# Two PSUM banks of the attention logits for the first products behind a k-outer group, and products and weight splits pinned to their pair or head chunk

## The chip, the cores and the metric

The kernel runs on one core of a Trainium2 chip. The metric is the device time of one execution in microseconds (us), lower is better: 987.88 us is the median of three runs of the kernel before (987.56 to 987.98).

## The reference

Two transformer blocks over 256 tokens of width 1024, in float32. The first mixes by a linear recurrence, gated linear attention and block-sparse attention, and ends in a SwiGLU with 2816 hidden units (22 columns of 128). The second has a convolution layer and an attention layer, each followed by a SwiGLU of the same size, with shifts, scales and gates from a vector c (adaLN). Cut to what matters here:

```python
def first_block(x, ...):
    x = x + rms_norm(hybrid_mixer(rms_norm(x, g0), ...) @ w_out, g1)
    h = rms_norm(x, g2)
    f = (silu(h @ w_ffn_gate) * (h @ w_ffn_up)) @ w_ffn_down          # ffn0
    return x + rms_norm(f, g3)

def second_block(x, c, ...):
    for l in range(2):
        sh1, sc1, g1, sh2, sc2, g2 = split(silu(c) @ w_ada[l] + b_ada[l], 6)
        h = x * (1 + sc1) + sh1
        if l == 0:
            gb, gc, v = split(h @ w_in, 3)                             # conv
            y = (gb * conv3(gc * v)) @ w_out
        else:
            k, v, F = shared_kv(x, c, ...)                             # F: cumulated log forget gates
            logits = q @ k.T / 8 + F[t] - F[s]                         # causal, 16 heads
            y = (softmax(logits) @ v) @ w_o                            # FoX
        x = layer_norm(alpha * x + g1 * y, ...)
        h = x * (1 + sc2) + sh2
        y = (silu(h @ w_gate) * (h @ w_up)) @ w_down                   # ffn1, ffn2
        x = layer_norm(alpha * x + g2 * y, ...)
    return x
```

## The kernel before

All activations lie transposed: 8 tiles of 128 features x 256 tokens. A float32 product is made of three matmuls on TensorE (PE): a weight block of 128 x 128 is split into a high part wh and a low part wl, the activation into xh and xl (yh, yl and mh, ml elsewhere), and wh·xh, wl·xh and wh·xl are summed in PSUM (`mm3`, L162 to L164; `ksteps`, L197 to L203). Weights come in tiles of 128 x 1024 (512 KB, eight blocks): the SP queue loads `raw` (L127, 4 buffers), ScalarE (ACT) casts it to `wh` (L144) and VectorE (DVE) subtracts to get `wl` (L150); wh and wl have 5 buffers each. One such tile feeds 24 matmuls, which this text calls a block of PE work.

PSUM has eight banks, in three pools: `acc` 4, `lg` 2 and `ms` 2. `lg` holds the attention logits and the target of the warm-up products (`warm`, L331), `ms` statistics, broadcasts and transposes. Where a layer's input becomes ready tile by tile, `kouter` computes eight columns at once with the eight k-steps outside, in all four acc banks. After that, columns come one after the other: `pair` (a gate and an up column in one bank, 48 matmuls) in the SwiGLUs, `single` elsewhere. `evac` in `ffn` multiplies silu(gate) and up (L918; in ffn0 with a scaling first, L909 and L911, then L914), and splits the result into mh (L921, ACT) and ml (L922, DVE). Columns j of a SwiGLU after the k-outer group start at n + 4, n being the columns computed ahead (0 in ffn0, 3 in ffn1 and ffn2). In conv the eight columns of the group are the first of the order c, v, b of head 0, head 1 and so on; L1207 ff. take the others by `single`, and L1212, L1215 evacuate.

adaLN: silu(c) @ w_ada is done on DVE, a row of 1024 products with a running sum each (`gw`, L371, from a load of 512 KB, 3 buffers, L368). There are 112 of them, spread over the program by `fill` and `drain`.

The program is written in stages and a scheduler orders the instructions of each engine; what the text adds by hand are order-only dependencies (`after`). A gw comes behind the last wl that was emitted (`self.anchor`) and behind `self.gbound`, if set. `unbroken(ins, free)` sets `self.bound`: after `free` more weight tiles, each wl comes behind an instruction of `ins`; it sets gbound to the last of them.

FoX works through the 16 heads in eight chunks of two. For chunk i: the query columns of chunk i + 1 (`wq`), logits of chunk i (L773 to L781) in the two lg banks, the transposes of chunk i - 1 (`fox_pt`, L805 to L807, a_pt), two k-steps of the output projection (`step`, `out`), and the softmax of chunk i (`fox_softmax`): a maximum on DVE (L793), the exps on ACT with a running sum (L794), a reciprocal (L795) and the scaling a_L (L797). Its PE order is the program's. Before the loop all wl's are pinned behind one instruction, and after chunk 0 behind that and chunk 0's last maximum:

```python
                if i == 0:
                    self.unbroken([self.gbound, self.mxs], 0)
```

Of the kernel before, what the change touches and what calls it, by code (L numbers as in the profile page):

```python
# [9 lines left out]
F32 = mybir.dt.float32  # L10
# [4 lines left out]
ALU = mybir.AluOpType  # L15
AX = mybir.AxisListType

P = 128
D = 1024
T = 256  # L20
NK = D // P
# [43 lines left out]
class Net:  # L65
# [99 lines left out]
        if self.strict:  # L165
            self.chain(m)

    def single(self, wname, c, X, nk=NK, fill=True):
        t = self.acc([P, T])
        for k in range(nk):  # L170
            self.mm3(t, wname, k, c, X[0][k], X[1][k], k == 0, k == nk - 1)
        if fill:
            self.fill(nk / NK)
        return t

    def pair(self, w0, c0, w1, c1, X):
        t = self.acc([P, 2, T])
        for j, (w, c) in enumerate(((w0, c0), (w1, c1))):
            for k in range(NK):
                self.mm3(t[:, j, :], w, k, c, X[0][k], X[1][k], k == 0 and j == 0, k == NK - 1 and j == 1)  # L180
        self.fill(2)
        return t
# [601 lines left out]
    def fox_softmax(self, lg):  # L784

        V, A = self.nc.vector, self.nc.scalar
        mx = self.tmp("a_mx", (P, 4))
        sm = self.tmp("a_sm", (P, 4))
        Ls = [self.tmp("a_L", (P, 384), bufs=4) for _ in range(2)]
        part = [(hh, j, s) for hh in range(2) for j, s in ((0, slice(0, T)), (1, slice(T, 384)))]  # L790
        for hh, j, s in part:
            c = slice(2 * hh + j, 2 * hh + j + 1)
            self.mxs = V.tensor_reduce(mx[:, c], lg[hh][:, s], AX.X, ALU.max, negate=True)  # L793
            self.fn = A.activation(Ls[hh][:, s], lg[hh][:, s], AF.Exp, bias=mx[:, c], accum_out=sm[:, c])  # L794
        V.reciprocal(sm, sm)  # L795
        for hh, j, s in part:
            V.tensor_scalar(Ls[hh][:, s], Ls[hh][:, s], sm[:, 2 * hh + j:2 * hh + j + 1], None, ALU.mult)  # L797
        return Ls

    def fox_pt(self, Ls):  # L800
# [99 lines left out]
    def ffn(self, l, X, R=None, first=(), rows=None):  # L900

        nc = self.nc
        V = nc.vector
        MH, ML = [], []

        def evac(g, u):
            if R is not None:
                g2 = self.tmp("ff_g")
                V.tensor_tensor(g2, g, R, ALU.mult)  # L909
                u2 = self.tmp("ff_u")  # L910
                V.tensor_tensor(u2, u, R, ALU.mult)  # L911
                s = self.silu(g2)
                m = self.tmp("ff_m")
                V.tensor_tensor(m, s, u2, ALU.mult)  # L914
            else:
                s = self.silu(g)
                m = self.tmp("ff_m")
                V.tensor_tensor(m, s, u, ALU.mult)  # L918
            h = self.tl(self.fp, [P, T + 2], "mh", F32R)[:, 0:T]
            lo = self.tl(self.fp, [P, T + 2], "ml", F32R)[:, 0:T]  # L920
            nc.scalar.activation(h, m, AF.Copy)  # L921
            V.tensor_tensor(lo, m, h.bitcast(F32), ALU.subtract)  # L922
            MH.append(h)
            ML.append(lo)

        wg, wu = f"g{l}", f"u{l}"
        n = len(first) // 2
        for o in range(0, 2 * n, 4):
            outs = [self.tmp("ff_g" if q % 2 == 0 else "ff_u") for q in range(o, min(2 * n, o + 4))]
            self.lazy_outs(first[o:o + 4], *rows, outs)  # L930
            for j in range(0, len(outs), 2):
                evac(*outs[j:j + 2])
        for ps in self.kouter([(w, n + j) for j in range(4) for w in (wg, wu)], X, False):
            evac(ps[:, 0, :], ps[:, 1, :])
        for j in range(n + 4, NFF):
            ps = self.pair(wg, j, wu, j, X)
            self.drain()
            evac(ps[:, 0, :], ps[:, 1, :])
        return MH, ML
# [139 lines left out]
    def run(self):  # L1079
        nc = self.nc  # L1080
        V, A, G = nc.vector, nc.scalar, nc.gpsimd
# [6 lines left out]
        X = ([], [])  # L1088
# [58 lines left out]
        X = Y  # L1147
# [54 lines left out]
        got = {}  # L1202
# [4 lines left out]
        for i in range(NK):  # L1207
            for w in ("ci_c", "ci_v", "ci_b"):
                if (w, i) not in got:
                    got[(w, i)] = self.single(w, i, X)  # L1210
            c = self.tmp("c_c")
            A.activation(c, got[("ci_c", i)], AF.Copy)  # L1212
            up = self.tmp("c_up", (P, T + 2))
# [87 lines left out]
            for j, t in enumerate(self.fox_pv(i, pts, vs)):  # L1301
                Y[j].append(t)

        self.unbroken([self.gbound], 2)
        with self.tc.manual_schedule(engines={nc.tensor.engine}):
            q = wq(0)
            Ls = None
            step, pre = self.partial("wo")
            for i in range(NK + 1):
                qn = wq(i + 1) if i < NK - 1 else None  # L1310
                lg = self.fox_logits(i, q, ks[i]) if i < NK else None
                pts = self.fox_pt(Ls) if i else None
                if i > 1:
                    step(Y, i - 2)
                if i:
                    out(i - 1, pts)
                Ls = self.fox_softmax(lg) if i < NK else None
                if i == 0:
                    self.unbroken([self.gbound, self.mxs], 0)
                q = qn  # L1320
                self.drain()
            step(Y, NK - 1)
# [162 lines left out]
```

## Time and profile before

| | before |
|---|---|
| median of three runs | 987.88 us (987.56 to 987.98) |
| profiled execution | 985.9 us, of which the span of instructions is 984.2 |
| PE busy | 927.9 us, 94% |
| DVE busy | 768.8 us, 78% |
| ACT busy | 530.2 us, 54% |

The profile is of one execution. A row of a timeline gives start and length in us, engine, line, operation, what it writes and reads, and in brackets how long its engine stood idle before it and which instruction released it. Matmuls overlap, so their lengths are longer than their spacing. The granted clock is TensorE's, as a part of 2.4 GHz.

### The profile page before, as it was taken

To read this page: it belongs to the slowest core of one execution; us is meant where nothing else is said; L and a number is where in the kernel's file an instruction comes from. 1 tells how busy PE (TensorE), PEld (TensorE's weight loads), DVE (VectorE), ACT (ScalarE), POOL (GpSimd) and SP (SyncE) were. 2 spreads that over 40 slices of the span, in tenths; PEclk is the share of its full clock that TensorE was granted. 3 is DMA by queue.
4 is the path that set the end of the run, shared out by engine and by line. 5 is a ranking of instruction groups with operands and counts; after the bars stand their busy time and mean duration, and the time that the engine had idled before them with its cause. 6 is when DMAs were issued, how large, how long until landed. Compare 5 with 4: busy or idle time off the path is not lost.

```text
span 984.2 us, 19003 instructions
## 1 busy us (share of the span) xinstructions
PE 927.9 (94%) x7434; PEld 893.6 (91%) x7434; DVE 768.8 (78%) x1471; ACT 530.2 (54%) x951; POOL 19.7 (2%) x66
## 2 busy tenths in 40 slices
PE   7989997999999999998899999999699999999996
PEld 7879896999999899998899999987587899999995
DVE  7896678999988588679899899796764897665553
ACT  7484653554444555548555454377365586554331
POOL 1111000000000000000000000000000000000001
PEclk9999998999999999999999999999799999999998
DMA  8754337899999477544999999454642257655531
GB/s 291 249 197 129 108 108 278 294 330 327 318 336 390 142 255 250 179 134 155 320 341 356 329 368 348 167 176 145 250 150 65 87 153 275 214 184 183 191 108 43
DMA packets 62346, 219.56 MB, mean 223 GB/s; under 512 B 7112, under 2 KB 8784, under 8 KB 62256
## 3 DMA queue, kind: packets, MB, share of 16 engines
q1 hardware_dynamic: 61056, 215.06, 63.7%
q0 software_dynamic: 1056, 3.16, 1.0%
q8 instruction: 58, 0.95, 0.4%
q14 instruction: 32, 0.26, 0.1%
q10 hardware_dynamic: 144, 0.13, 0.0%
HBM read 217.26 MB, written 2.63 MB: 223 GB/s over the span
## 4 chain that ended last, share of the span: by engine, by line
PE 80%; DVE 12%; ACT 4%; issue 3%; DMA 2%; DVEq 0%; ACTq 0%
PE acc L162 20%; PE acc L164 20%; PE acc L163 20%; PE acc L197 4%; DVE wl L150 4%; PE acc L198 4%; PE acc L203 3%; DMA raw<-wts 1%; ACT wh L144 1%; DVE gw L371 1%; PE acc L251 1%; PE acc L253 1%; PE acc L252 1%; PE ms L820 1%; PE lg L773 1%
## 5 line engine op out<-in xcount | busy, mean ns | idle before, releaser
L150 DVE TENSOR_TENSOR wl<-raw,wh 128x1024 fp32r<-128x1024 f32 (+2 forms) x296 | 356.2, 1209 | 102.4 <-ACT wh L144 101.0
L144 ACT ACTIVATE wh<-raw 128x1024 fp32r<-128x1024 f32 (+2 forms) x296 | 307.6, 1046 | 225.4 <-PE acc L164 128.2
L162 PE MATMUL acc<-yh,wh 128*128 128x256 f32 x608 | 171.1, 282 | 7.0 <-DVE ff_m L918 5.6
L162 PE MATMUL acc<-xh,wh 128*128 128x256 f32 x576 | 164.2, 285 | 8.9 <-DVE ff_u L911 7.2
L164 PE MATMUL acc<-yl,wh 128*128 128x256 f32 x608 | 171.3, 282 | 0.0
L163 PE MATMUL acc<-yh,wl 128*128 128x256 f32 x608 | 170.6, 281 | 0.0
L163 PE MATMUL acc<-xh,wl 128*128 128x256 f32 x576 | 162.9, 283 | 1.4 <-DVE wl L150 1.4
L164 PE MATMUL acc<-xl,wh 128*128 128x256 f32 x576 | 163.0, 283 | 0.0
L163 PE MATMUL acc<-mh,wl 128*128 128x256 f32 x528 | 148.1, 281 | 0.0
L164 PE MATMUL acc<-ml,wh 128*128 128x256 f32 x528 | 148.1, 281 | 0.0
L162 PE MATMUL acc<-mh,wh 128*128 128x256 f32 x528 | 147.9, 281 | 0.0
L371 DVE SCALAR_TENSOR_TENSOR gw<-gw,cact 128x1024 f32<-128x1024 f32 x112 | 134.7, 1221 | 0.6 <-DMA gw<-ada 0.4
L162 PEld LDWEIGHTS acc<-yh,wh 128*128 128x128 f32 x608 | 115.2, 190 | 7.6 <-DVE ff_m L918 6.1
L162 PEld LDWEIGHTS acc<-xh,wh 128*128 128x128 f32 x576 | 109.9, 191 | 11.3 <-DVE ff_u L911 7.4
L163 PEld LDWEIGHTS acc<-yh,wl 128*128 128x128 f32 x608 | 115.2, 190 | 0.4 <-issue 0.4
L164 PEld LDWEIGHTS acc<-yl,wh 128*128 128x128 f32 x608 | 114.9, 189 | 0.6 <-issue 0.6
L163 PEld LDWEIGHTS acc<-xh,wl 128*128 128x128 f32 x576 | 110.1, 191 | 1.8 <-DVE wl L150 1.6
L164 PEld LDWEIGHTS acc<-xl,wh 128*128 128x128 f32 x576 | 109.8, 191 | 0.1
L162 PEld LDWEIGHTS acc<-mh,wh 128*128 128x128 f32 x528 | 99.5, 189 | 0.0
L164 PEld LDWEIGHTS acc<-ml,wh 128*128 128x128 f32 x528 | 99.4, 189 | 0.0
L163 PEld LDWEIGHTS acc<-mh,wl 128*128 128x128 f32 x528 | 99.3, 188 | 0.0
L197 PE MATMUL acc<-xh,wh 128*128 128x256 f32 (+1 forms) x256 | 67.7, 294 | 8.7 <-ACT wh L144 5.5
(399 smaller groups left out, 1493.2 us busy)
## 6 DMA issues: line engine op xcount, KB each, us to landing
raw<-wts SPq DMA_DIRECT2D x288, 512.0 KB, 4.5
gw<-ada SPq DMA_DIRECT2D x112, 512.0 KB, 5.6
raw<-wts SPq DMA_DIRECT2D x6, 256.0 KB, 5.9
m_scr<-m_row POOLq DMA_DIRECT2D x2, 768.0 KB, 5.8
ax<-xT SPq DMA_DIRECT2D x4, 256.0 KB, 4.8
m_b<-m_scr POOLq DMA_DIRECT2D x8, 128.0 KB, 3.6
out<-fg SPq DMA_DIRECT2D x8, 128.0 KB, 1.8
cst<-cst SPq DMA_DIRECT2D x1, 588.5 KB, 7.1
```

Source lines behind the costliest of these rows:

```text
L144: i = self.aw = nc.scalar.activation(self.wh[:, d], r, AF.Copy)
L150: self.anchor = nc.vector.tensor_tensor(self.wl[:, d], r, self.wh[:, d].bitcast(F32), ALU.subtract)
L162: m = [mm(ps, wh, xh, start=start, stop=False), mm(ps, wl, xh, start=False, stop=False), mm(ps, wh, xl, start=False, stop=stop)]
L163: mm(ps, wl, xh, start=False, stop=False),
L164: mm(ps, wh, xl, start=False, stop=stop)]
L197: m.append(mm(outs[i], wh, X[0][k], start=k == 0 and i % per == 0, stop=False))
L198: m.append(mm(outs[i], wl, X[0][k], start=False, stop=False))
L203: m.append(mm(outs[i], wh, X[1][k], start=False, stop=False))
L251: mm(outs[tt], h, wh, start=k == 0 and (tt == 0 or not one), stop=False)
L252: mm(outs[tt], l, wh, start=False, stop=False)
L253: mm(outs[tt], h, wl, start=False, stop=k == NK - 1 and (tt == 1 or not one))
L371: i = nc.vector.scalar_tensor_tensor(t, t, 1.0, self.cact, op0=ALU.mult, op1=ALU.mult, accum_out=self.ada[:, g:g + 1])
```

## The change

`single` and `pair` get a flag `spare`: with it the result goes into an lg bank and not an acc bank. In a SwiGLU the two pairs behind the k-outer group take it (j = 4, 5 in ffn0; 7, 8 in ffn1 and ffn2), in conv the ninth and tenth column (`order[8:10]`). `evac` sets gbound to its last instruction, ml, so every later gw comes behind the ml of the pair before. In FoX gbound and bound follow the chunks: of what is emitted after chunk i's softmax, gw's come behind the last scaling (`self.alast`) of chunk i and wl's behind that of chunk i - 1. Lines from L1301 on move by one (L1372 becomes L1373).

```diff
-    def single(self, wname, c, X, nk=NK, fill=True):
-        t = self.acc([P, T])
+    def single(self, wname, c, X, nk=NK, fill=True, spare=False):
+        t = self.tl(self.plg, [P, T], "lg") if spare else self.acc([P, T])
...
-    def pair(self, w0, c0, w1, c1, X):
-        t = self.acc([P, 2, T])
+    def pair(self, w0, c0, w1, c1, X, spare=False):
+        t = self.tl(self.plg, [P, 2, T], "lg") if spare else self.acc([P, 2, T])
...
         for hh, j, s in part:
-            V.tensor_scalar(Ls[hh][:, s], Ls[hh][:, s], sm[:, 2 * hh + j:2 * hh + j + 1], None, ALU.mult)
+            self.alast = V.tensor_scalar(Ls[hh][:, s], Ls[hh][:, s], sm[:, 2 * hh + j:2 * hh + j + 1], None, ALU.mult)
...
-            V.tensor_tensor(lo, m, h.bitcast(F32), ALU.subtract)
+            self.gbound = V.tensor_tensor(lo, m, h.bitcast(F32), ALU.subtract)
...
-            ps = self.pair(wg, j, wu, j, X)
+            ps = self.pair(wg, j, wu, j, X, j < n + 6)
...
-                    got[(w, i)] = self.single(w, i, X)
+                    got[(w, i)] = self.single(w, i, X, spare=(w, i) in order[8:10])
...
-        self.unbroken([self.gbound], 2)
+        al = self.gbound
+        self.unbroken([al], 2)
...
-                if i == 0:
-                    self.unbroken([self.gbound, self.mxs], 0)
+                if i < NK:
+                    self.bound, self.gbound, al = [al], self.alast, self.alast
```

How the instructions move, at three places. In the names, the number is that of the buffer's allocation, wl_2127 and wl_2157 are the weights of the gate and up column of ffn0's first pair, wl_2203 and wl_2233 of its second.

DVE at the start of ffn0's pairs, behind the k-outer group, in the kernel before:

```order
L150 TENSOR_TENSOR wl_2127<-raw_2124,wh_2126 128x1024
L150 TENSOR_TENSOR wl_2157<-raw_2154,wh_2156 128x1024
L371 SCALAR_TENSOR_TENSOR gw_2184,ada_175<-gw_2184,cact_1825 128x1024
L150 TENSOR_TENSOR wl_2203<-raw_2200,wh_2202 128x1024
L150 TENSOR_TENSOR wl_2233<-raw_2230,wh_2232 128x1024
L371 SCALAR_TENSOR_TENSOR gw_2260,ada_175<-gw_2260,cact_1825 128x1024
L371 SCALAR_TENSOR_TENSOR gw_2263,ada_175<-gw_2263,cact_1825 128x1024
L909 TENSOR_TENSOR ff_g_2075<-acc_1831,R_394_1823 128x256
```

The same place in the changed kernel:

```order
L150 TENSOR_TENSOR wl_2127<-raw_2124,wh_2126 128x1024
L150 TENSOR_TENSOR wl_2157<-raw_2154,wh_2156 128x1024
L150 TENSOR_TENSOR wl_2203<-raw_2200,wh_2202 128x1024
L150 TENSOR_TENSOR wl_2233<-raw_2230,wh_2232 128x1024
L909 TENSOR_TENSOR ff_g_2075<-acc_1831,R_394_1823 128x256
L911 TENSOR_TENSOR ff_u_2077<-acc_1831,R_394_1823 128x256
```

The three gw's are gone from this place; they stand some 25 rows later, behind the evacuation's ml's.

DVE between ffn0 and conv, from the root of the post-norm (L279 to L289) to conv's first inputs (L1191, L1192, L267), in the kernel before:

```order
L279 TENSOR_SCALAR nw_v_4301<-ms_4200 128x2
L288 SCALAR_TENSOR_TENSOR nw_q_4296<-nw_y_4292,nw_v_4294 128x1 x2
L289 SCALAR_TENSOR_TENSOR nw_y_4297<-nw_q_4296,nw_y_4292 128x2
L288 SCALAR_TENSOR_TENSOR nw_q_4303<-nw_y_4297,nw_v_4301 128x1 x2
L289 SCALAR_TENSOR_TENSOR nw_y_4304<-nw_q_4303,nw_y_4297 128x2
L1191 TENSOR_TENSOR fg_3615<-fg_3615,ms_4308 128x256
```

And in the changed kernel:

```order
L279 TENSOR_SCALAR nw_v_4301<-ms_4200 128x2
L288 SCALAR_TENSOR_TENSOR nw_q_4296<-nw_y_4292,nw_v_4294 128x1 x2
L289 SCALAR_TENSOR_TENSOR nw_y_4297<-nw_q_4296,nw_y_4292 128x2
L288 SCALAR_TENSOR_TENSOR nw_q_4303<-nw_y_4297,nw_v_4301 128x1
L371 SCALAR_TENSOR_TENSOR gw_4096,ada_175<-gw_4096,cact_1825 128x1024
L288 SCALAR_TENSOR_TENSOR nw_q_4303<-nw_y_4297,nw_v_4301 128x1
L289 SCALAR_TENSOR_TENSOR nw_y_4304<-nw_q_4303,nw_y_4297 128x2
L1191 TENSOR_TENSOR fg_3615<-fg_3615,ms_4308 128x256
L371 SCALAR_TENSOR_TENSOR gw_4099,ada_175<-gw_4099,cact_1825 128x1024
L1192 TENSOR_TENSOR ax_92<-ax_92,fg_3615 128x256
L1191 TENSOR_TENSOR fg_3714<-fg_3714,ms_4308 128x256
L371 SCALAR_TENSOR_TENSOR gw_4102,ada_175<-gw_4102,cact_1825 128x1024
```

gw_4096, gw_4099 and gw_4102 were ahead of the statistics and now stand among the steps.

DVE in FoX, from behind chunk 0's maxima (a_mx_8912) to its scales (a_L_8914, a_L_8915), in the kernel before:

```order
L793 TENSOR_REDUCE a_mx_8912<-lg_8897 128x1
L150 TENSOR_TENSOR wl_9022<-raw_9019,wh_9021 128x1024
L371 SCALAR_TENSOR_TENSOR gw_9049,ada_175<-gw_9049,cact_1825 128x1024
L371 SCALAR_TENSOR_TENSOR gw_9052,ada_175<-gw_9052,cact_1825 128x1024
L150 TENSOR_TENSOR wl_9088<-raw_9085,wh_9087 128x1024
L150 TENSOR_TENSOR wl_9146<-raw_9143,wh_9145 128x1024
L371 SCALAR_TENSOR_TENSOR gw_9161,ada_175<-gw_9161,cact_1825 128x1024
L795 RECIPROCAL a_sm_8913<-a_sm_8913 128x4
L150 TENSOR_TENSOR wl_9237<-raw_9234,wh_9236 128x1024
L793 TENSOR_REDUCE a_mx_9000<-lg_8963 128x1
L150 TENSOR_TENSOR wl_9303<-raw_9300,wh_9302 128x1024
L793 TENSOR_REDUCE a_mx_9000<-lg_8964 128x1
```

There two gw's and then the four scales follow; a_mx_9000 are maxima of chunk 1. In the changed kernel:

```order
L793 TENSOR_REDUCE a_mx_8912<-lg_8897 128x1
L795 RECIPROCAL a_sm_8913<-a_sm_8913 128x4
L797 TENSOR_SCALAR a_L_8914<-a_L_8914,a_sm_8913 128x256
L797 TENSOR_SCALAR a_L_8914<-a_L_8914,a_sm_8913 128x128
L797 TENSOR_SCALAR a_L_8915<-a_L_8915,a_sm_8913 128x256
L797 TENSOR_SCALAR a_L_8915<-a_L_8915,a_sm_8913 128x128
L150 TENSOR_TENSOR wl_9022<-raw_9019,wh_9021 128x1024
L150 TENSOR_TENSOR wl_9088<-raw_9085,wh_9087 128x1024
```

The five wl's and five gw's that stood between maxima and scales come behind the scales of this or a later chunk. ACT at the same place in the changed kernel, from behind chunk 1's queries (a_q_8894), with wh the casts and a_L the exps:

```order
L144 ACTIVATE wh_9236<-raw_9234 128x1024
L794 ACTIVATE a_L_8914,a_sm_8913<-lg_8896,a_mx_8912 128x256
L794 ACTIVATE a_L_8915,a_sm_8913<-lg_8897,a_mx_8912 128x256
L794 ACTIVATE a_L_8914,a_sm_8913<-lg_8896,a_mx_8912 128x128
L794 ACTIVATE a_L_8915,a_sm_8913<-lg_8897,a_mx_8912 128x128
L1297 ACTIVATE a_q_8961<-acc_8930 128x256
L809 ACTIVATE a_pt_8983<-ms_8979 128x384
L809 ACTIVATE a_pt_8989<-ms_8985 128x384
L794 ACTIVATE a_L_9002,a_sm_9001<-lg_8963,a_mx_9000 128x256
L794 ACTIVATE a_L_9003,a_sm_9001<-lg_8964,a_mx_9000 128x256
L266 ACTIVATE yh_8996<-ms_8991 128x256
L794 ACTIVATE a_L_9002,a_sm_9001<-lg_8963,a_mx_9000 128x128
```

In the kernel before, wh_9236 and wh_9302 stood behind chunk 0's last exp and ahead of chunk 1's first; now the first of them is ahead of chunk 0's exps, and wh_9302 comes some rows further down, ahead of the last exp of chunk 1.

## Rows read from the trace of the kernel before

**Rows 1.** The page, part 1: busy us, share of the span, instructions.

```profile
PE 927.9 (94%) x7434; PEld 893.6 (91%) x7434; DVE 768.8 (78%) x1471; ACT 530.2 (54%) x951; POOL 19.7 (2%) x66
```

**Rows 2.** Timeline of PE: start, length, line, operation, tiles, [idle before, releaser].

```profile
164.46 0.58 PE L162 MATMUL acc<-xh,wh 128*128 128x256 f32 x1 [7.24 <-DVE ff_u L911]
...
330.73 0.28 PE L162 MATMUL acc<-mh,wh 128*128 128x256 f32 x1
...
330.97 0.28 PE L164 MATMUL acc<-ml,wh 128*128 128x256 f32 x1
...
360.76 0.39 PE L162 MATMUL acc<-xh,wh 128*128 128x256 f32 x1 [1.10 <-DVE c_up L1215]
...
478.47 0.39 PE L162 MATMUL acc<-yh,wh 128*128 128x256 f32 x1 [3.68 <-DVE ff_m L918]
...
701.83 0.48 PE L805 MATMUL ms<-ident,a_L 128*128 128x128 f32 x1 [9.50 <-DVE a_L L797]
...
709.75 0.92 PE L773 MATMUL lg<-f_k,a_q 64*128 64x256 f32 x8
...
774.86 0.39 PE L197 MATMUL acc<-xh,wh 128*128 128x258 f32 x1 [2.26 <-DVE fg L972]
...
821.65 0.38 PE L162 MATMUL acc<-yh,wh 128*128 128x256 f32 x1 [1.97 <-DVE ff_m L918]
```

**Rows 3.** Windows: length, busy us of PE, PEld, DVE, ACT, POOL, clock, DMA share, GB/s.

```profile
166.00:168.00 2.00, 2.00 (x11) 2.00 (x11) 2.00 (x7) 1.43 (x4) 0.00 (x0) 0.50 1.01 408
...
168.00:170.00 2.00, 2.00 (x16) 2.00 (x15) 1.85 (x6) 0.81 (x3) 0.00 (x0) 0.78 0.99 395
...
334.00:336.00 2.00, 1.89 (x10) 1.38 (x10) 1.31 (x4) 1.33 (x2) 0.00 (x0) 1.00 0.00 0
...
480.00:482.00 2.00, 2.00 (x11) 2.00 (x11) 2.00 (x6) 0.00 (x0) 0.00 (x0) 0.50 1.04 420
...
482.00:484.00 2.00, 2.00 (x16) 2.00 (x15) 1.20 (x4) 1.62 (x3) 0.00 (x0) 0.77 1.03 399
...
704.00:706.00 2.00, 2.00 (x10) 1.27 (x9) 0.53 (x3) 0.37 (x2) 0.00 (x0) 0.50 0.98 391
...
776.00:778.00 2.00, 2.00 (x13) 2.00 (x12) 1.79 (x6) 0.80 (x2) 0.00 (x0) 0.61 0.53 197
...
778.00:780.00 2.00, 2.00 (x8) 1.48 (x7) 0.33 (x1) 0.00 (x0) 0.00 (x0) 0.53 0.04 8
```

**Rows 4.** Timeline of DVE around ffn0's first evacuations.

```profile
155.67 2.36 DVE L150 TENSOR_TENSOR wl<-raw,wh 128x1024 fp32r<-128x1024 f32 x2
...
157.94 1.22 DVE L371 SCALAR_TENSOR_TENSOR gw<-gw,cact 128x1024 f32<-128x1024 f32 x1
...
163.65 0.43 DVE L909 TENSOR_TENSOR ff_g<-acc,R 128x256 f32<-128x256 f32 x1
```

**Rows 5.** Timeline of DVE and PE from ffn0's statistics to conv's first matmul.

```profile
332.37 0.16 DVE L276 TENSOR_SCALAR nw_y<-ms 128x2 int32<-128x2 int32 x1 [6.38 <-PE ms L299]
...
336.64 0.39 PE L197 MATMUL acc<-xh,wh 128*128 128x256 f32 x1 [0.75 <-ACT xh L266]
```

**Rows 6.** Timeline of DVE, ACT and the SP queue at FoX's first chunk.

```profile
681.39 0.68 DVE L842 TENSOR_TENSOR_SCAN f_F<-f_z,ls_l 16x256 f32<-16x256 f32 x1 [2.88 <-ACT ls_l L838]
...
687.54 3.17 SPq L127 DMA_DIRECT2D raw<-wts  x2
...
689.48 0.19 ACT L794 ACTIVATION_READ_ACCUMULATOR a_L<-lg,a_mx 128x1 f32 x1
...
692.39 1.06 ACT L144 ACTIVATE wh<-raw 128x1024 fp32r<-128x1024 f32 x1 [2.71 <-DMA raw<-wts]
...
701.22 1.01 DVE L797 TENSOR_SCALAR a_L<-a_L,a_sm 128x256 f32<-128x256 f32 x4
```

**Rows 7.** Timeline of DVE at FoX's last two chunks.

```profile
745.82 1.01 DVE L797 TENSOR_SCALAR a_L<-a_L,a_sm 128x256 f32<-128x256 f32 x4
...
749.60 0.87 DVE L793 TENSOR_REDUCE a_mx<-lg 128x1 f32<-128x256 f32 x2 [1.22 <-PE lg L781]
```

## The prediction

> **What bounds the kernel now.** The page comes first [rows 1]: TensorE (PE) is busy 94% of the span, so time is to be had only where PE stands still or runs at half clock. PE's timeline then gives each stop with its releaser [rows 2]. Five touch this change: 7.24 us at ffn0's first pair (released by the evacuation's ff_u), 1.10 in the conv mixer (c_up), 3.68 at ffn1's first pair (ff_m), 9.50 in FoX (the softmax scale a_L), 1.97 at ffn2's first pair (ff_m). Windows of 2 us [rows 3] add the clock: after the long stops 0.50 is granted, 1.2 instead of 2.4 GHz. Last comes VectorE (DVE) behind the stops. At ffn0 it does wl's from 155.67, then a gw, and the first ff_g only at 163.65 [rows 4]; its order before has two wl's, a gw, two wl's and two gw's there. In FoX chunk 0's last exp ends at 689.67 and its scales come at 701.22 [rows 6], with wl's and gw's between them in the order. So what binds at these places is the order on DVE, not its load.
>
> **The change, part by part.** Durations come from one execution of 985.9 us (span 984.2), 2.0 us under the median of 987.88; the sum is made on it. The instructions stay the same in number; places and banks move.
>
> ffn0. The first two pairs write the two lg banks, so PE needs no evacuation for four blocks of weights. A block is 24 matmuls at 0.12 us (330.73 to 330.97 are two steps [rows 2]): 2.9 us. The stop began at 164.46 - 7.24 = 157.2. DVE's new order has wl_2127, 2157, 2203 and 2233 in a row. At 1.14 each (155.67 to 157.94 are two; a gw is as long, 1.22 beside 2.36 for two wl's [rows 4]) from 155.67 they end at 156.8, 157.9, 159.1 and 160.2; PE wants them at 157.2, 160.1, 163.0 and 165.9. The first bank's two evacuations follow, done by 161.1 (at 0.43 each, the length of ff_g [rows 4]); the third pair wants it at 168.7. So 7.24 goes, and the half clock behind it: 164.46 to 168 at 0.50 (its second window is shown) and 2.0 us at 0.78 lose 1.77 + 0.44 = 2.2 [rows 3]. Sum 9.4.
>
> conv: the ninth and tenth column take the lg banks, the stop goes: 1.1. ffn1: 3.68 and the clock of 480 to 484, 1.0 + 0.46 [rows 3]: 5.1. ffn2: 1.97, with no clock loss counted: 2.0. In both the four wl's already stand ahead of the evacuations in the new order, so nothing else is late.
>
> The gw's. All 112 stay. A pair's gw's now come only behind the previous pair's ml, so they run later in ffn0, and the new order has gw_4096 between two steps of the post-norm's root and gw_4099 between conv's first L1191 and its L1192. Before, this stretch has no gw: root, broadcast, L1191, L1192, ln_w, first matmul at 336.64, each waiting for the one ahead [rows 5]. So 2 x 1.14 = 2.3 lie on the path; gw_4102, behind that L1192, meets only the second k-step, due 2.9 us later. The ends are 0 (if the gw's fit into waits after all) and 4.6 (if a gw's transfer is late by as much again); I take 2.3, the nearest to the row. From ffn1 to FoX one gw now stands ahead of an xl: 0 to 1.1, taken as 0.5.
>
> The clock at ffn0's end. PE fills the waits with warm-up products; the window of 334 to 336 shows 1.89 of 2 us busy and a clock of 1.00 [rows 3]. The only like case is the stop of 2.26 us before 774.86 [rows 2]; 0.61 and 0.53 behind it lose 0.8 + 0.9 = 1.7 [rows 3]. One gw lengthens a hole by 1.14, half of 2.26, so I take no loss; the loss is rival B. The Trainium skill (TensorE: Matmul & The Clock Gate, Part 1: The HAM clock gate) has the clock follow how busy PE has been recently; by that rule the thinner stretch may fall to half, and the sum would be 1.7 worse. The trace agrees with the rule at 776 to 780; whether the stretch here is thin enough no row shows.
>
> FoX. wl's and gw's are pinned behind the previous chunk's scales, so chunk 0's maxima, reciprocal and scales stand together on DVE. Alone this would remove the 9.50 and the half clock of 702 to 708 (three windows at 0.50, the middle one shown, 3.0 [rows 3]): 12.5. But ScalarE (ACT) now has wh_9236 ahead of chunk 0's exps and wh_9302 ahead of chunk 1's last exp, and both wait for their raw tiles (wh_9236 did so before, for 2.71 [rows 6]). A raw tile is issued when an older wl frees its buffer: 687.54, cast from 692.39, 4.85 later. In the new order ACT's ls_y and ls_l come ahead of casts and copies that they stood behind, so DVE's wait of 2.88 [rows 6] for ls_l goes, and some 1.4 more for the two casts ahead of ls_y, less wl_8867, which now stands among the gates. I take 4.3 in all: the wl that freed the buffer at 687.4 (the issue at 687.54 is behind it [rows 6]) ends at 683.1. So wh_9236 runs from 688.0 to 689.0, the exps (1.8) to 690.9, the scales to 691.9; the first transpose, L805, stands at 692.1 instead of 701.83. wl_9022 ends at 693, raw_9300 is cast from 697.8, chunk 1's last exp ends at 699.6, and chunk 2's logits start at 700.0; before, 709.75 [rows 2]. That is 9.7, with its two new waits paid. Later chunks run as before, but casts stand ahead of a copy a_pt or an exp: 0.7 taken (bounds 0 and 4.5, one wait for raw as above in each of four chunks). At the end four wl's (4.56) stand between chunk 6's scales, done at 746.83, and chunk 7's maxima, which were at 749.60: 751.4, and of these 1.8 I take 1.5 as reaching PE [rows 7]. FoX: 9.7 - 0.7 - 1.5 = 7.5, between 0 and 12.5.
>
> Sum: 9.4 + 1.1 + 5.1 + 2.0 + 7.5 - 2.3 - 0.5 = 22.3. 985.9 - 22.3 = 963.6, plus 2.0: **965.6 us**.
>
> **Rivals.** A: FoX gains nothing, as casts ahead of exps wait for raw tiles in every chunk. For it: the wait of 2.71 [rows 6]. Against: five chunks lie between 709.75 [rows 2] and 749.60 [rows 7], just under 8 us each, against 4.85 for a tile. 965.6 + 7.5 = 973.1.
> B: the clock falls at ffn0's end: 965.6 + 1.7 = 967.3.
> C: weights hold the first pairs in place of banks. For it: transfers take 0.99 to 1.04 of the DMA engines in the windows there [rows 3]. Against: the four wl's were done before 163.65 even with gw's between them [rows 4], and PE wants the last at 165.9. If half of ffn0's and ffn1's 14.5 stays: 965.6 + 7.3 = 972.9.
> D, the other side: deferred gw's take the place of the wl that PE wants next. A pair of ffn0 is 5.8 us of PE; on DVE it is two wl's (2.3), four evacuating operations (1.7 at 0.43) and about 1.5 gw's (1.7), 5.7 together, so what is put off has little room to be caught up. One gw on the path in each of some 45 pairs would be 51 us: 965.6 + 51 = 1017. It decides from 20 pairs on (20 x 1.14 = 22.8). Against it: DVE idles 6.38 us at ffn0's end [rows 5], so it is not short of time over ffn0 as a whole.
> That the change does nothing is excluded by the new order.
>
> **How the numbers follow.** Forecast 0.64 (own range 959 to 971), A 0.17, B 0.08, C 0.06, D 0.05. The low end is FoX whole (5.0 more) and nothing lost at ffn0's end (2.3) or behind ffn1 (0.5): 957.8, so 957. The high end is A with B's 1.7 and the late transfer's 2.3: 977.1, so 977. Within 0.2%, 2 us, is about what a measurement of this kernel cannot tell from no change. Faster 0.93; same 0.02 and slower 0.05, D near and beyond its point.
>
> **What would show it.** Right: no stop of PE over 0.3 us and a clock of 1.00 at the first pairs of ffn0, ffn1 and ffn2; FoX's first L805 10 us earlier against the logits ahead of it; some 2.3 us more between ffn0's last product and conv's first. Wrong: stops on wl or raw inside the first two pairs (C), on a_L or a_pt once a chunk (A), on wl all over the pairs (D).

## The result, and the profile of the changed kernel

The changed kernel takes 957.06 us (median of 3 runs, 956.40 to 957.59) against 987.88: a ratio of 0.9688, with a 95% interval of 0.9666 to 0.971. That is 30.8 us less, where 22.3 were forecast. The profiled execution took 957.06 as well, with a span of 955.4. The page's part 1 of the changed kernel stands against [rows 1]:

```profile
PE 918.4 (96%) x7434; PEld 886.5 (93%) x7434; DVE 766.8 (80%) x1471; ACT 527.4 (55%) x951; POOL 19.8 (2%) x66
```

The instructions are as many as before, and DVE's and ACT's work is as long to within 0.6%. PE lost 9.5 us of busy time; the rest of the 28.8 us of span is standing time. (Between the medians it is 30.8, as the profiled execution before lies 2.0 under its median and this one on it.) To see where, I cut both traces at events that both have. The table (us, made from timelines, not a view of the profile) gives each stretch: "mixer" is all up to DVE's last step of the root (L289) ahead of ffn0; "ffn0" runs to its statistics (L299), "bound" from there to conv's first product, "conv" to ffn1's first waiting product, "ffn1" to the stop on wl at L253 that both kernels have ahead of FoX, "FoX" to its last output product that waits for yh.

```
                  before    after    measured   forecast
mixer             155.60   157.63      +2.03       0
ffn0              176.12   166.72      -9.40     -9.4
bound               4.92     7.09      +2.17     +2.3
conv              112.49   110.47      -2.02     -1.1
ffn1, way to FoX  203.27   198.13      -5.14     -4.6  (-5.1 +0.5)
FoX               109.00    95.82     -13.18     -7.5
norm behind FoX    13.46    13.45      -0.01       0
ffn2, ahead        23.00    21.79      -1.21       0
ffn2              172.76   170.53      -2.23     -2.0
sum                                   -28.99    -22.3
```

PE's timeline of the changed kernel (start, length, line, tiles, idle before and releaser) answers to [rows 2]:

```profile
158.65 0.40 PE L162 MATMUL lg<-xh,wh 128*128 128x256 f32 x2
...
327.68 0.68 PE L308 MATMUL ms<-ident,nw_y 128*128 128x128 f32 x4 [1.31 <-DVE nw_y L289]
...
331.44 0.38 PE L197 MATMUL acc<-xh,wh 128*128 128x256 f32 x1 [1.77 <-ACT xh L266]
...
678.24 0.27 PE L805 MATMUL ms<-ident,a_L 128*128 128x128 f32 x1
...
684.42 0.92 PE L773 MATMUL lg<-f_k,a_q 64*128 64x256 f32 x6 [0.22 <-ACT a_L L794]
...
749.31 0.38 PE L197 MATMUL acc<-xh,wh 128*128 128x258 f32 x1 [2.25 <-DVE fg L972]
```

At 158.65 the first pair of ffn0 goes into a bank named lg, and there is no idle time before it; at the ninth columns of conv and at the first pairs of ffn1 and ffn2 the timeline has no stop either. In FoX the transposes of chunk 0 at 678.24 stand 6.5 us behind that chunk's logits (671.75); before it was 17.7 (684.12 to 701.83). What is new are the waits at 327.68, ahead of the broadcast of the root, 1.31 where 0.17 stood, and at 331.44, 1.77 where 0.75 stood [rows 5]: 2.2 us more together. Windows of 2 us (columns as in [rows 3]) give the clock:

```profile
158.00:160.00 2.00, 2.00 (x19) 2.00 (x19) 2.00 (x3) 0.38 (x1) 0.00 (x0) 1.00 0.27 70
...
166.00:168.00 2.00, 2.00 (x19) 2.00 (x18) 1.59 (x3) 2.00 (x5) 0.00 (x0) 1.00 0.98 358
...
326.00:328.00 2.00, 0.69 (x5) 0.35 (x4) 1.50 (x5) 1.50 (x2) 0.00 (x0) 1.00 0.00 0
...
330.00:332.00 2.00, 0.56 (x4) 0.57 (x5) 2.00 (x5) 1.02 (x2) 0.00 (x0) 1.00 0.48 111
...
732.00:734.00 2.00, 2.00 (x12) 2.00 (x11) 0.00 (x0) 0.49 (x1) 0.00 (x0) 0.50 0.23 84
...
750.00:752.00 2.00, 2.00 (x19) 2.00 (x18) 1.81 (x5) 0.84 (x2) 0.00 (x0) 1.00 0.64 209
```

Full clock at ffn0's first pairs, where 0.50 was granted before; full clock also between ffn0 and conv, though PE was busy for only 0.69 and 0.56 of 2 us there. Half clock stays at FoX's end (732), as it did before.

DVE's timeline shows the order doing what its list said. At ffn0's start, at ffn0's end and in FoX:

```profile
157.71 4.62 DVE L150 TENSOR_TENSOR wl<-raw,wh 128x1024 fp32r<-128x1024 f32 x4
162.25 0.42 DVE L909 TENSOR_TENSOR ff_g<-acc,R 128x256 f32<-128x256 f32 x1
...
325.00 0.16 DVE L276 TENSOR_SCALAR nw_y<-ms 128x2 int32<-128x2 int32 x1 [4.14 <-PE ms L299]
...
325.98 1.22 DVE L371 SCALAR_TENSOR_TENSOR gw<-gw,cact 128x1024 f32<-128x1024 f32 x1
...
328.74 1.22 DVE L371 SCALAR_TENSOR_TENSOR gw<-gw,cact 128x1024 f32<-128x1024 f32 x1
...
662.64 0.67 DVE L842 TENSOR_TENSOR_SCAN f_F<-f_z,ls_l 16x256 f32<-16x256 f32 x1
...
667.48 1.22 DVE L150 TENSOR_TENSOR wl<-raw,wh 128x1024 fp32r<-128x1024 f32 x1
...
676.69 1.01 DVE L797 TENSOR_SCALAR a_L<-a_L,a_sm 128x256 f32<-128x256 f32 x4
```

Four wl's, then the evacuations; two gw's of 1.14 us on the way to conv, inside a stretch that is 2.17 longer; and in FoX the scan L842 without the wait of 2.88 for ls_l that it had [rows 6]. FoX as a whole stands 12.37 us earlier now (671.75 against 684.12 for chunk 0's logits). With that added, which this text calls the old scale, the scan starts at 675.0 instead of 681.39.

### The profile page after: what moved, and what is told of

Its sections match the earlier page's. It is cut to its first block, busy times and chain, and to the rows that moved or that the text cites. A ratio compares the mean times of both kernels' runs of the same rounds, so it can differ in the third digit from the quotient of the medians.

```text
span 955.4 us, 18971 instructions
## 1 busy us (share of the span) xinstructions
PE 918.4 (96%) x7434; PEld 886.5 (93%) x7434; DVE 766.8 (80%) x1471; ACT 527.4 (55%) x951; POOL 19.8 (2%) x66
## 4 chain that ended last, share of the span: by engine, by line
PE 81%; DVE 10%; DMA 3%; ACT 3%; issue 2%; SPq 0%; DVEq 0%; ACTq 0%
PE acc L162 19%; PE acc L164 19%; PE acc L163 18%; PE acc L197 4%; PE acc L198 4%; PE acc L203 4%; DVE wl L150 3%; DMA raw<-wts 2%; PE lg L164 1%; PE lg L162 1%; PE lg L163 1%; PE acc L253 1%; PE acc L251 1%; PE acc L252 1%; ACT wh L144 1%
## 5 line engine op out<-in xcount | busy, mean ns | idle before, releaser
L162 PE MATMUL acc<-yh,wh 128*128 128x256 f32 x544 | 152.3, 280 | 0.9 <-ACT yh L266 0.9
L164 PE MATMUL acc<-yl,wh 128*128 128x256 f32 x544 | 152.6, 281 | 0.5 <-DVE yl L267 0.5
L163 PE MATMUL acc<-yh,wl 128*128 128x256 f32 x544 | 151.9, 280 | 0.0
L162 PE MATMUL acc<-xh,wh 128*128 128x256 f32 x528 | 148.8, 282 | 0.3 <-ACT g_v L654 0.3
L164 PE MATMUL acc<-xl,wh 128*128 128x256 f32 x528 | 148.3, 281 | 0.0
L163 PE MATMUL acc<-xh,wl 128*128 128x256 f32 x528 | 147.9, 280 | 0.0
L162 PEld LDWEIGHTS acc<-yh,wh 128*128 128x128 f32 x544 | 102.3, 188 | 1.1 <-ACT yh L266 1.1
L164 PEld LDWEIGHTS acc<-yl,wh 128*128 128x128 f32 x544 | 102.1, 188 | 0.8 <-DVE yl L267 0.7
L163 PEld LDWEIGHTS acc<-yh,wl 128*128 128x128 f32 x544 | 102.5, 189 | 0.0
L163 PEld LDWEIGHTS acc<-xh,wl 128*128 128x128 f32 x528 | 99.5, 188 | 0.2
```

The lines of the kernel that those rows point to most:

```text
L162: m = [mm(ps, wh, xh, start=start, stop=False), mm(ps, wl, xh, start=False, stop=False), mm(ps, wh, xl, start=False, stop=stop)]
L163: mm(ps, wl, xh, start=False, stop=False),
L164: mm(ps, wh, xl, start=False, stop=stop)]
```

## The experiments

The change has three parts: the spare banks in single and pair (S), the pin of ffn's gw's behind ml (G), and the pins inside FoX (F). My prediction gave ffn0, conv, ffn1 and ffn2 to S alone, saw in G only the cost at ffn0's end, and gave FoX to F with some help of G's order. The first six runs take the parts one by one. Where a ratio is given it is to the kernel before on the same chip, whose medians were 987.57 (first four), 986.34 (next four) and 987.24 (last three).

**S alone.** Edit against the kernel before:

```diff
-        t = self.acc([P, 2, T])
+        t = self.tl(self.plg, [P, 2, T], "lg") if spare else self.acc([P, 2, T])
...
-            ps = self.pair(wg, j, wu, j, X)
+            ps = self.pair(wg, j, wu, j, X, j < n + 6)
```

and the same in single, with conv's call.

> Only the two lg banks for the first pairs and for conv's ninth and tenth column; no pin of the gw's, no change in FoX. Theory (banks pay at the starts, the pin of the gw's only costs between ffn0 and conv): the first pairs' stops go in ffn0, ffn1 and ffn2 and in conv, 9.4 + 5.1 + 2.2 + 2.0 = 18.7 less than before, and no gw between ffn0's statistics and conv's first product, so that stretch is as before: 988 - 18.7 = 969. Rival (deferring the gw's is what frees the first pairs, the banks are incidental): under 5 us gained, 983 or more, with a stop on wl or ff_u at ffn0's first pairs.

Measured: 977.74 (976.44 to 980.08), 0.9899 [0.9876, 0.9922], between the theory's 969 and the rival's 983. conv, ffn1 and ffn2 gain what they gain in the whole change (-2.0, -5.5 and -2.1 us), but ffn0 takes 175.91, 0.2 less than before. PE has no stop at the first pair, and instead, 40 us later, on PE's timeline and in a window behind it:

```profile
202.11 0.55 PE L162 MATMUL acc<-xh,wh 128*128 128x256 f32 x1 [6.27 <-DVE ff_u L911]
```

```profile
204.00:206.00 2.00, 2.00 (x11) 2.00 (x11) 2.00 (x7) 1.33 (x4) 0.00 (x0) 0.50 0.91 358
```

DVE's timeline of the same run says why:

```profile
159.13 0.16 DVE L276 TENSOR_SCALAR nw_y<-ms 128x2 int32<-128x2 int32 x1 [3.18 <-PE ms L299]
...
197.80 1.21 DVE L371 SCALAR_TENSOR_TENSOR gw<-gw,cact 128x1024 f32<-128x1024 f32 x1
...
198.94 1.21 DVE L371 SCALAR_TENSOR_TENSOR gw<-gw,cact 128x1024 f32<-128x1024 f32 x1
...
201.56 0.41 DVE L911 TENSOR_TENSOR ff_u<-acc,R 128x256 f32<-128x256 f32 x1
...
208.70 1.23 DVE L150 TENSOR_TENSOR wl<-raw,wh 128x1024 fp32r<-128x1024 f32 x1 [1.49 <-ACT wh L144]
```

Between 159.13 and 208.70 no row of DVE has an idle time before it: the engine is full for 50 us. The two banks let PE run ahead, DVE does not catch up, and when the banks are used up PE waits for an ff_u that stands behind two gw's. The stop was put off, not removed. How much of DVE's time the gw's take in that stretch is one window with the filter on that tile (length, DVE's busy time on it and rows, ACT's, clock, DMA share, GB/s), for S alone and then for the changed kernel:

```profile
160.00:203.00 43.00, 14.42 (x24) 0.00 (x0) 0.94 0.94 333
```

```profile
160.00:203.00 43.00, 9.47 (x15) 0.00 (x0) 1.00 0.88 300
```

With the pin 4.95 us fewer of gw's lie in these 43 us; they come later in ffn0, where DVE has gaps. (ffn0's pairs start 2.7 us earlier in the changed kernel; from the same point of ffn0, 157.27 to 200.27, its gw's take 8.46, 5.96 fewer.) Read with the stop of 6.27, that is most of what PE had waited for.

How full DVE is does not tell the cases apart. In those 43 us it is busy 42.97 us with the banks alone and 42.15 in the changed kernel, which has no stop; in 43 us of ffn1 with the banks alone (474.70 to 517.70) it is busy 42.37, and there the stop does not come back either. How far DVE runs behind PE does tell. From the end of a pair's products to the end of its ff_u it takes 23.6, 21.3 and 23.0 us for ffn0's first three pairs with the banks alone (the third's is the ff_u at 201.56 above), and 9.8, 6.0 and 4.3 in the changed kernel; in ffn1 with the banks alone, where ff_m frees the bank, 13.1, 7.8 and 7.7, and then 4.7 and less.

**G alone.**

```diff
-            V.tensor_tensor(lo, m, h.bitcast(F32), ALU.subtract)
+            self.gbound = V.tensor_tensor(lo, m, h.bitcast(F32), ALU.subtract)
```

> Only the pin of each gw behind the ml of the pair before. Theory: the evacuation at ffn0's start comes after four wl's instead of four wl's and three gw's, so the stop of 7.24 falls to about 3.8 with less half clock behind it, ffn1's of 3.68 to about 2.5 or less, ffn2's stays: 4 to 8 us gained, 980 to 984. Rival (the pin is what pays): ffn0's and ffn1's stops are gone, some 15 us gained, 973.

Measured: 978.85 (975.68 to 980.76), 0.9904 [0.9877, 0.9931], 1 us under the theory's range. A pin alone, with the old banks, is worth 9 us: ffn0 -3.8, ffn1 -3.6, FoX -3.6 (mostly clock, see below). It shortens the stop at ffn0's first pair, since the gw's are no longer ahead of the evacuation, but PE still needs that bank:

```profile
163.17 0.38 PE L162 MATMUL acc<-xh,wh 128*128 128x256 f32 x1 [3.80 <-DVE ff_u L911]
```

The stretch behind ffn0 stays at 4.90: here the last gw is done at 326.67, ahead of the statistics at 330.74, so it takes banks and pin together to push gw's past them. FoX's gates are early: the stop on wl at L253 stands at 647.20 here and at 652.40 before, so FoX stands 5.2 earlier, and the scan L842, at 669.82, is at 675.0 on the old scale, as in the changed kernel. But early gates are not what shortens FoX here. Its stop on a_L remains:

```profile
695.74 0.48 PE L805 MATMUL ms<-ident,a_L 128*128 128x128 f32 x1 [10.19 <-DVE a_L L797]
```

S with G, further down, has the scan as early and the same stop of 10.19, and its FoX takes 108.39 against 105.39 here. The difference is clock. Two windows of this run, one behind that stop and one at FoX's end, and then the same two of S with G:

```profile
698.00:700.00 2.00, 2.00 (x12) 1.36 (x11) 0.44 (x2) 0.39 (x1) 0.00 (x0) 0.63 0.99 401
750.00:752.00 2.00, 2.00 (x13) 1.08 (x12) 0.00 (x0) 0.00 (x0) 0.00 (x0) 1.00 0.89 238
```

```profile
694.00:696.00 2.00, 2.00 (x11) 2.00 (x11) 0.42 (x1) 0.00 (x1) 0.00 (x0) 0.50 0.17 68
744.00:746.00 2.00, 2.00 (x11) 2.00 (x11) 0.66 (x2) 0.49 (x1) 0.00 (x0) 0.50 0.37 72
```

Half clock behind the stop loses 1.9 us here and 3.1 there, and at FoX's end nothing here and 1.7 there: 3.0 together. So 3.0 of the 3.6 are clock, and the early gates alone are worth 0.6.

**F alone.** With alast set as in the change:

```diff
...
-        self.unbroken([self.gbound], 2)
+        al = self.gbound
+        self.unbroken([al], 2)
...
-                if i == 0:
-                    self.unbroken([self.gbound, self.mxs], 0)
+                if i < NK:
+                    self.bound, self.gbound, al = [al], self.alast, self.alast
```

> Only FoX's pins chunk by chunk. Theory: the stop of 9.50 and the half clock behind it go, 13 us gained as in the changed kernel's trace, 975; the other stops are as before. Rival (FoX's gain in the changed kernel needs the gw's to be late when they arrive there): under 9 us, 979 or more.

Measured: 983.21 (982.11 to 983.89), 0.9948 [0.993, 0.9966]; FoX gains 4.9. The rival's number holds; its reason, gw's that have to arrive late, does not, as the sixth run gets FoX's whole gain with ffn's gw's where they were. DVE's scan is as late as before, and ACT then stands at casts whose raw tiles have not landed, with exps and copies behind them. DVE, ACT and PE:

```profile
683.46 0.68 DVE L842 TENSOR_TENSOR_SCAN f_F<-f_z,ls_l 16x256 f32<-16x256 f32 x1 [2.66 <-ACT ls_l L838]
```

```profile
694.17 1.06 ACT L144 ACTIVATE wh<-raw 128x1024 fp32r<-128x1024 f32 x1 [2.43 <-DMA raw<-wts]
...
697.68 1.06 ACT L144 ACTIVATE wh<-raw 128x1024 fp32r<-128x1024 f32 x1 [1.11 <-DMA raw<-wts]
...
699.59 0.47 ACT L809 ACTIVATE a_pt<-ms 128x384 f32<-128x384 f32 x1
```

```profile
696.63 0.65 PE L820 MATMUL ms<-a_pt,ax 128*64 128x256 f32 x2 [1.58 <-ACT a_pt L809]
700.12 1.54 PE L820 MATMUL ms<-a_pt,ax 128*64 128x256 f32 x6 [2.84 <-ACT a_pt L809]
```

The stop on a_L is gone, and two stops on a_pt have come, 4.4 together, with half clock from 698 to 706. This is my rival A, in two chunks rather than in all.

**S with F, and S with G.** The edits are those above, in pairs.

> Banks and FoX, without the pin of the gw's. Theory: all gains of the changed kernel and none of the 2.2 us between ffn0 and conv, so about 2 us under the changed kernel: 955. Rival (without the pin gw's stand ahead of wl's or evacuations that PE wants in the pairs): 958 or more, with new stops in the first pairs.

Measured: 974.03 (971.09 to 975.24), 0.9854 [0.9829, 0.9879], against 957 for all three: the rival holds, and what is missing is G. ffn0 has its stop of 6.27 again at 201.59 (175.32 for the stretch), and FoX gains 3.2.

> Banks and the pin of the gw's, FoX's pins as in the kernel before. Theory (the pin at the starts also brings FoX's gates forward, by some 3.6 us as with the pin alone, and only FoX's own pins remove the stop on a_L): FoX's stretch from the last stop on a wv weight to the last stop on yh about 105.4 us, 9.6 longer than the changed kernel's 95.8, everything else as there: 957 + 9.6 = 966.7. Rival (the pin alone puts FoX in order once the banks are there): 960 or less.

Measured: 969.42 (967.41 to 971.65), 0.983 [0.9805, 0.9854]. ffn0, bound, conv and ffn1 are those of the whole change to 0.02 us (166.72, 7.08, 110.47, 198.14); FoX takes 108.39, with the stop on a_L of 10.19; the 105.4 expected was G alone's, and the 3.0 by which it missed are the clock shown there. So S and G together carry everything outside FoX, and F all but 0.6 us of FoX's gain, but only with G there.

**Does F need G's pin, or only early gates?** F alone, with the casts of the third tile of queries on pinned behind the gate's last activation, ls_l:

```diff
-        A.activation(ln, u, AF.Ln)
+        self.lsl = A.activation(ln, u, AF.Ln)
...
-        self.unbroken([al], 2)
+        self.unbroken([al], 2, [self.lsl])
```

> FoX's pins alone as in e3, and in addition the casts of the query weights from the third on come behind ls_l on ACT, so that the gates are done earlier; no banks, no pin of the gw's. Theory (what FoX's pins lacked in e3 was the early gates: then older wl's end earlier, raw tiles are issued earlier and casts no longer stand waiting ahead of the copies a_pt): FoX's stretch goes from 104.1 us in e3 to 96 to 98, 975 to 977. Rival (the missing 8 us come from the gw's that the other pin moves): no more than 2 us under e3, 981 or more.

Measured: 973.47 (971.47 to 977.13), 0.9875 [0.9849, 0.99]. FoX takes 93.95, with neither S nor G. DVE's scan has no wait any more (FoX stands 1.5 later here, so it is at 677.5 on the old scale, 3.9 earlier), and ACT's two casts wait less than in F alone. DVE, then ACT:

```profile
679.01 0.68 DVE L842 TENSOR_TENSOR_SCAN f_F<-f_z,ls_l 16x256 f32<-16x256 f32 x1
```

```profile
690.04 1.06 ACT L144 ACTIVATE wh<-raw 128x1024 fp32r<-128x1024 f32 x1 [0.62 <-DMA raw<-wts]
...
695.52 1.06 ACT L144 ACTIVATE wh<-raw 128x1024 fp32r<-128x1024 f32 x1 [0.41 <-DMA raw<-wts]
```

So what F lacks is that ACT does ls_y and ls_l ahead of the weight casts; then the casts' tiles are asked for sooner (the first load is issued at 685.10 and not at 689.61, 3.8 us sooner behind the stop at L253), and 0.62 and 0.41 stand where 2.43 and 1.11 stood. The theory holds, with FoX 2 us under the 96 to 98 expected. ACT's order moves with the pin too: both copies a_pt stand ahead of the second cast here (692.55 and 692.94), where F alone had one behind it. How much that order adds to the earlier tiles no run separates. (1.7 of this run's gain is FoX's end at full clock, which the changed kernel does not have; without it FoX would stand at 95.7, where it stands there.) Why pinning ffn's gw's makes the scheduler put the two activations forward is not shown by any run.

**The price at ffn0's end.** The changed kernel with its last three gw's of ffn0 pinned behind the inputs of conv:

```diff
+            self.gws.append(i)
...
+        for i in self.gws[-3:]:
+            self.after(i, steps[-1][2])
         self.pipeline(steps)
```

> The changed kernel, with the last three gw's ahead of conv pinned behind the last xl of conv's inputs. Theory (two gw's lie on the path from ffn0's statistics to conv's first product): that stretch shrinks from 7.09 us in the changed kernel to 4.9 as before, and nothing is late later: 957 - 2.2 = 954.9. Rival (three gw's more in conv hold c_up or a wl): the 2.2 come back as stops in conv, 957.

Measured: 954.62 (953.43 to 955.98), 0.968 [0.9664, 0.9695]. The stretch to conv's first product is 4.92 again, so the 2.17 were the two gw's. But conv takes 112.52, 2.05 more, with a stop that the changed kernel has not:

```profile
360.76 0.39 PE L163 MATMUL acc<-xh,wh 128*128 128x256 f32 x1 [1.77 <-ACT c_c L1216]
```

The rival holds: the cost has moved. The median is 2.4 lower nevertheless, but against the kernel before on the same chip the ratio, 0.968, is within 0.001 of the changed kernel's 0.9688; in the profiles, the mixer is 1.8 shorter (155.86 instead of 157.63, last section) and FoX 0.8 (94.98).

**FoX's end.** The changed kernel with the five wl's at FoX's end, on DVE, pinned one by one: two behind chunk 6's scales as before, one behind chunk 7's last maximum and two behind its scales:

```diff
+                if i == NK - 1:
+                    self.unbroken([self.bound[0]] * 2 + [self.mxs, self.alast], 0)
```

> The changed kernel, with the five weight splits at FoX's end pinned one by one: two behind chunk 6's scales, one behind chunk 7's last maximum, two behind chunk 7's scales. Theory (four splits hold chunk 7's maxima by 1.5 us and the fifth its reciprocal by 1.7): both go, 2.5 to 3.2 us, and if the clock stays up behind them another 1.7: 952 to 954.5. Rival (the output projection's products behind FoX wait for the splits instead): 957, with a stop on wl there.

Measured: 953.28 (952.72 to 955.42), 0.9673 [0.9654, 0.9692]. FoX takes 92.40, 3.4 less; the theory holds. On DVE of the changed kernel, then of this one:

```profile
720.98 4.63 DVE L150 TENSOR_TENSOR wl<-raw,wh 128x1024 fp32r<-128x1024 f32 x4
...
725.85 0.75 DVE L793 TENSOR_REDUCE a_mx<-lg 128x1 f32<-128x256 f32 x2
```

```profile
720.36 2.35 DVE L150 TENSOR_TENSOR wl<-raw,wh 128x1024 fp32r<-128x1024 f32 x2
...
722.97 0.75 DVE L793 TENSOR_REDUCE a_mx<-lg 128x1 f32<-128x256 f32 x2
```

The maxima follow the scales after 3.5 us, not after 5.8, and the window of 732 to 734 has a clock of 1.00 instead of 0.50. Of the 3.4, 1.7 are clock: 0.77, 0.50 and 0.87 in the three windows from 730 of the changed kernel lose 0.46 + 1.0 + 0.26. That half is not surely the edit's: the sixth run has the same stops at FoX's end as the changed kernel (0.94, 0.47 and 0.28 ahead of its last products) and no half clock there, and nor do F alone and S with F, with much the same stops. But the three profiles with this edit have none, and the three that share the changed kernel's order at FoX's end (its own two and the seventh run's) all have it.

**Both, and a better place for the gw's.** The tail's edit, and the three gw's one by one behind the yl's of conv's first three output columns:

```diff
+        late = self.gws[-3:]
...
             h, l = self.hilo(y, "y")
+            if late:
+                self.after(late.pop(0), self.lo)
```

> The changed kernel with e8's pins at FoX's end, and the last three gw's ahead of conv pinned one each behind the yl of conv's first three output columns (in e7 all three stood in a row ahead of c_up and gave their 2.2 us back). Theory: ffn0's end 4.9 us instead of 7.1, conv 110.5 without a stop, FoX 92.4 as in e8: 5.6 under the changed kernel, 951.5. Rival (a gw in conv costs its length wherever it stands there): 953.5, with conv at 112.5.

Measured: 951.93 (949.94 to 954.59), 0.9641 [0.9619, 0.9663]: the fastest version by median and ratio, though its interval overlaps that of the tail alone. The stretch to conv is 4.92, and conv takes 111.96, between the theory's 110.5 and the rival's 112.5, with one stop of 1.21 on c_y: 0.7 net for the gw's, and the tail's gain stays (FoX 91.43).

> e9 with e6's pin of the casts behind ls_l. Theory (the gates of the changed kernel are early enough): FoX within 1 us of e9, 951.5. Rival (with every cast behind the gates FoX gains a further 1.9 us, as e6's 93.95 against the changed kernel's 95.82): 949.5.

Here ls_l's pin (the edit of the sixth run) is added to that. Measured: 953.56 (951.62 to 955.74), 0.9656 [0.9636, 0.9676]: nothing more, and the rival's 949.5 is not reached; the gates are early already. FoX takes 92.80, 1.4 over the run before, so not within the 1 us expected, and conv has two stops instead of one (113.08).

> The changed kernel again, on the chip of e9 and e10, to compare them with: 957, with the same stretches from ffn0 on as in its first profile, and a stretch ahead of ffn0 that differs with where TensorE's clock falls in it (155.5 to 160.4 us in the profiles so far, whose order there is the same).

The changed kernel without an edit, on the same chip as the last two. Measured: 955.24 (953.66 to 957.96), 0.9675 [0.9655, 0.9696]. The best version is 3.3 us under it by medians; their ratios' intervals just overlap, but the stretches carry the same sign: -2.2 at ffn0's end, +1.5 in conv, -4.3 from FoX to the norm behind it.

## Why the prediction was right, and where it was not

The forecast of 965.6 had the sign, the places and most of the mechanism; one cause (ffn0) and one size (FoX) were wrong. 957.06 lies 0.06 above the low end of the range, 957, and outside the 959 to 971 that I gave as the forecast's own. That it lies inside at all is luck: the repeat of the changed kernel took 955.24, on a chip where the kernel before took 987.24.

**ffn0** (-9.4; -9.40) is met, stop and clock. Its stated cause is not: I gave it to the banks, by counting DVE's next six operations. S alone gives 0.2 and G alone 3.8; only both give 9.40. The step that failed is "So 7.24 goes", as far as it was argued from the first two pairs: with the banks alone the first pairs have no stop either, and 6.27 comes back 40 us later. That the sum came out to 0.1 all the same is in part luck. Rival D had the number for what follows, 5.7 us of DVE work in a pair of 5.8 us, but I read it as a danger of the deferral; it is the reason why the deferral is needed. The banks let PE run two pairs ahead, once, and a DVE that does not catch up gives the wait back.

**ffn1 and ffn2** (-5.1 and -2.0; -5.14 with the way to FoX, and -2.23) are met, and there the banks alone do it: -5.5 and -2.1 in the first run. **conv** (-1.1; -2.02) lacked the second stop of 0.38 on c_c at 364.23 of the trace before, also gone, and some 0.5 in holes and lengths too small for a row.

**The boundary** (+2.3; +2.17) is met: two gw's of 1.14 on the path. The 0.5 taken for a gw ahead of an xl between ffn1 and FoX shows as 0.4, and at another place: with G the stretch is 198.14, with the banks alone 197.76, and the stop on wl at L253 is 1.19 instead of 0.69, as another operation (L1073) stands between two wl's there. Rival B fell: the clock stayed at 1.00 through windows with 0.69 and 0.56 of 2 us busy. The rule of the Trainium skill that I had weighed there (TensorE: Matmul & The Clock Gate, Part 1: The HAM clock gate), that the clock follows how busy PE has been, would have allowed a fall, and the trace did not show one. A did not come in the changed kernel, where no stop on a_pt or a_L in FoX is over 0.64; it came in F alone. C fell, as no first pair stops on weights. D did not come: the deferred gw's found room.

**FoX** (-7.5; -13.18) is the term that was mis-sized, by 5.7, in two places. First, "I take 4.3 in all" for the gates: they came 6.4 earlier (681.39 against 675.0 on the old scale), and so did the wl that frees a buffer, which ends at 668.62 + 12.37 = 681.0, not 683.1. Of the 6.4, 4.5 are what I had counted: from f_z (L835) on ACT to the scan it is 3.2 us instead of 7.7. The other 1.9 I had at nothing: f_z itself stands 19.4 us behind the stop at L253, not 21.3. Why, no run isolates. From there the chain ran as I had it, with its two waits for raw. On ACT:

```profile
673.65 1.06 ACT L144 ACTIVATE wh<-raw 128x1024 fp32r<-128x1024 f32 x1 [1.42 <-DMA raw<-wts]
...
682.47 1.06 ACT L144 ACTIVATE wh<-raw 128x1024 fp32r<-128x1024 f32 x1 [0.49 <-DMA raw<-wts]
```

The casts start at 686.0 and 694.8 on the old scale, where I had 688.0 and 697.8; the first tile took 5.0 us from the end of the wl that freed its buffer to its cast (668.62 to 673.65), the second 3.7 (678.75 to 682.47), where I had used 4.85 for both. Chunk 2's logits end 13.0 earlier (685.34 + 12.37 against 710.67), not 9.7: 3.3 of the miss. Second, the 0.7 for later chunks and the 1.5 for the tail: chunks 2 to 6 follow each other every 7.7 us, as before, and from the end of chunk 2's logits to FoX's last output it is 50.5 us against 50.7. The tail does cost, up to 3.4 by the run that mends it, but the kernel before lost there too, at 0.50 and 0.66 of the clock from 756 to 760; that row I had not read. Together 3.3 + 0.7 + 1.5 + 0.2 = 5.7.

**Not in the forecast**: +2.03 in the mixer and -1.21 ahead of ffn2. 1.7 of the first and all of the second are clock, in stretches where the change touches nothing; the last section shows them. The other 0.3 of the first lies ahead of 70 us, also in a stretch with the same order.

## What to carry to other kernels

In this kernel a spare PSUM bank removed a stop where the engine that evacuates caught up afterwards (read pair by pair in ffn1; in conv and ffn2 no stop came back either), and only put it off where that engine did not (ffn0). So look past the first waits at how far it runs behind, pair by pair; its busy share does not tell. If it does not catch up, put work that nobody waits for behind the evacuations along with the bank. Deferred work comes out somewhere, and the place it comes out at has to be read from the order like the place it left. Before pinning weight casts ahead of a softmax on the same engine, see that what frees their buffers runs early enough, or the softmax inherits the wait for the transfer.

## What the runs showed of the hardware

The same stop is followed by half clock in one run and not in another. The stop of 2.25 ahead of the product at 749.31 had 1.00 behind it in the changed kernel (shown above); the same program in its repeat, with the same stop (2.24, at 749.08), has in its windows

```profile
750.00:752.00 2.00, 2.00 (x14) 2.00 (x13) 1.79 (x6) 0.83 (x2) 0.00 (x0) 0.66 0.55 193
752.00:754.00 2.00, 2.00 (x8) 1.53 (x8) 0.55 (x2) 0.00 (x0) 0.00 (x0) 0.50 0.03 10
```

as the kernel before had behind its stop of 2.26 [rows 2, 3]. That is the 1.2 us ahead of ffn2, and no gain of the change. In the mixer, where all kernels have one order, the stretch took from 155.56 to 160.36 us over all profiles. In the kernel before, half clock fell here:

```profile
70.00:72.00 2.00, 2.00 (x9) 1.62 (x10) 1.96 (x5) 0.75 (x4) 0.32 (x1) 0.50 0.43 131
72.00:74.00 2.00, 1.53 (x4) 0.73 (x3) 2.00 (x10) 1.12 (x5) 0.00 (x0) 0.67 0.29 57
```

and in the changed kernel here:

```profile
76.00:78.00 2.00, 2.00 (x10) 1.74 (x9) 2.00 (x11) 0.99 (x4) 1.15 (x2) 0.50 0.43 107
78.00:80.00 2.00, 2.00 (x14) 2.00 (x14) 1.96 (x11) 1.36 (x5) 0.00 (x0) 0.71 0.41 98
```

Both lose about 1.7 us of clock, but at 70 to 74 PE next waits for ACT's yh until 74.33 in any case (74.64 in the changed kernel), while behind 76 to 80 the stretch ends 1.7 later: there, as I read it, the slow products are themselves the path. The fastest version's profile has no window under 0.99 up to 930 us, with the same two stops (2.41 and 2.37) at this place. The Trainium skill (TensorE: Matmul & The Clock Gate, Part 1: The HAM clock gate) says that the window in which the monitor behind the clock looks runs on freely and is not reset when a kernel starts; the repeat of one program with and without the fall agrees with that, and does not prove it. So differences of 2 us between kernels are, in this program, to be looked for in the stretch that an edit touches before they are believed.
